# Weight sums of two more pairs kept in DRAM, the leftover GpSimd jobs run under the output projection, and attention's transposes placed inside the next chunk's products

## The chip, the cores and the metric

The kernel runs on one core of a Trainium2 chip. The metric is the device time of one execution, in microseconds (us). The kernel before takes 1067.46 us as the median of 3 runs (1066.02 to 1068.29).

The engines of the core have short names in everything below: PE is TensorE (matrix products and transposes), DVE is VectorE, ACT is ScalarE, POOL is GpSimd, and SP is the engine whose queue issues most of the DMA transfers. Each engine works through its own list of instructions in order, and waits on the others by semaphores. L235 is line 235 of the kernel before, unless a line is said to be of the kernel after.

## What is computed

One encoder layer over 1024 positions of 1024 features, all in fp32:

```python
def reference(x, ...):
    h = rmsnorm(x, norm_mix_pre)
    y = mixer(h, w_in, conv_a, ...)            # 8 groups of short convolution, 4 heads of gated linear attention
    x = x + rmsnorm(y @ w_out, norm_mix_post)  # (w_out is inside mixer)
    h = rmsnorm(x, norm_ffn_pre)
    u = dwconv3(h @ w_up, conv_ffn)            # 1024 -> 2 * 2816, then a convolution of width 3 over positions
    gate, val = split(u)
    y = (silu(gate) * val) @ w_down            # 2816 -> 1024
    return x + rmsnorm(y, norm_ffn_post)
```

Attention works in chunks of 64 positions, forward and backward: a chunk's decayed keys `k_out` times its values give a state update `kv`, the states are scanned along the chunks, and the output is the masked scores times the values plus the queries times the state before.

## The kernel before, in words

Every fp32 operand of a large product is split into a high and a low part (ACT copies the high part, DVE subtracts to get the low part), and a product is three passes on PE: high by high, high by low, low by high. The whole program is bound to PE's list, which runs through these stages:

- **Start, 0 to 111 us.** Norm of x, its transposes (`hT`), the projection to V, and four output gates (`swish_gate`).
- **Attention and short convolution, 111 to 326 us.** `gla_head` (a generator, L474 on) is run for four heads, and its parts are interleaved with `conv_tile`, whose large products (`pgc`, `pgv`, `pgb`) are made by `feature_chunk` (L226 on): eight k-steps of 6 matmuls each, and after every k-step one entry of the list `between` is taken off and called. `gla_head` puts the state products (`states`) and the scores into that list. Two kinds of transposes on PE stand outside it: the decayed keys (`cum`, made by DVE at L514) are transposed into `pko` (L519) and copied to `koT`; the normed head output (`on`, made by DVE at L616) is transposed into `pot` (L622) and multiplied into `yT` by DVE.
- **The border, 326 to 440 us.** `w_out_tile(t)` multiplies one tile of 128 rows by w_out (PE, 8 tiles), then ACT and DVE norm it twice; `h2_transpose(t)` turns the result for the next stage. The weights of the up projection's first pairs are loaded and split here (`begin`, which makes `ug0h` and `ug0l` and so on).
- **Up projection, 440 to 849 us.** 22 pairs of a gate block and a value block, `up(c)`, pair c from 0 to 21. A pair is made by a scheme of seven block products instead of eight, each of 12 matmuls of 128x512, and needs four sums of weight blocks, s1 to s4. ACT, DVE and POOL prepare pair c+1 while PE works on pair c. DVE has besides the splits the additions of products into `cg` and `cv` (L1015, L1029, L1032, L1040, L1043), which read a bank of PE's output and free it for the next product, the convolution (L990, L991), the product of gate and value (L1066), and for odd pairs four sums (L1078 to L1082) of the activations, stored to DRAM.
- **Down projection, 849 to 1059 us**, a scheme of seven products too, over activations and weight sums in DRAM; then the last norm.

Where the weight sums come from: `jobs` is a list of 15 side jobs for POOL. Four of them (`up_begin`, `up_end`) load blocks of w_up, make four sums of 128x512 and store them to DRAM (`wu_d`), for pairs 0 to 3. Eleven (`down_begin`, `down_end`) do the same for w_down. `side()` starts one job and ends the one begun before. It is called during the start and the output gates; at L1160 a `while jobs` loop runs the three that are left, after the first product of the down projection. Pairs 0 to 3 (`N_EARLY = 4`) load their sums in `begin_sums`. For pairs 4 to 21 `make_sums(c)` (L868 on) loads the two full blocks (`ug4r`, `uv4r` for pair 4) and POOL makes the sums `us40r`, `us41r` (L880 to L883) two pairs ahead, in `up(c - 2)`.

A name as `us3al` is read so: weight sums of pair 3, s2 and s3 (`a`; `b` is s1 and s4), low part. `us30r` and `us31r` are the raw fp32 sums.

Of the kernel before, what the change touches and what calls it, by code (L numbers as in the profile page):

```python
# [40 lines left out]
def kernel(  # L41
# [39 lines left out]
    def ps_tile(name):  # L81
        return psp.tile([P, 1024], F32, tag="ps", name=name)
# [21 lines left out]

    def up_end(k, ag, av):
# [25 lines left out]

    def late_tile(name):
        return sp.tile([P, D], F32, tag="r", name=name)

    jobs = [(up_begin, up_end, i) for i in range(4)] + [(down_begin, down_end, q) for q in range(NQ)]

# [142 lines left out]
    with ExitStack() as n1:  # L279
# [133 lines left out]
        nc.tensor.transpose(pp[:, P : P + NPB], stk[0:NPB, 1, :], ident[0:NPB, 0:NPB])  # L413
        nc.vector.tensor_copy(prm, pp[:, 0 : P + NPB])

# [20 lines left out]
    nc.sync.dma_start(out=up_raw[RANK : 2 * RANK, :, DK:P], in_=gate_up_bwd[0].rearrange("r (h d) -> r h d", d=DK))  # L436
    nc.vector.tensor_copy(up96[0:32], up_raw)
    nc.vector.tensor_copy(up96[32:64], up_raw)
    nc.vector.tensor_sub(up96[64:96], up_raw, up96[0:32].bitcast(F32))

# [24 lines left out]
    def unit(tag, name, dt=F32, bufs=1):  # L465
        return mp.tile([P, L], dt, tag=tag, name=name, bufs=bufs)
# [8 lines left out]
    def gla_head(h):  # L475
# [40 lines left out]

        pk = ps_tile(f"pko{h}")
        for t in range(NT):
            nc.tensor.transpose(pk[:, t * P : (t + 1) * P], cum[:, t * P : (t + 1) * P], ident)  # L519
        koT = unit("koT", f"koT{h}")  # L520
        nc.scalar.copy(koT, pk)
# [22 lines left out]
        def states(i):  # L544
# [73 lines left out]

        pt = ps_tile(f"pot{h}")
        ptv = pt.rearrange("p (a b c i) -> p a b c i", b=2, c=2, i=CH)  # L620
        for s in range(NT):
            nc.tensor.transpose(ptv[:, s % 4, :, s // 4, :], on[:, s * P : (s + 1) * P], ident)  # L622
        nc.vector.scalar_tensor_tensor(yT[4 + h], pt, g_head, yT[4 + h], op0=ALU.mult, op1=ALU.mult)

# [370 lines left out]
    def up(c, before=iter(())):  # L995
# [268 lines left out]
```

## Time and profile before

| | |
|---|---|
| median of 3 runs | 1067.46 us (1066.02 to 1068.29) |
| the profiled execution: its own time | 1067.92 us |
| the profiled execution: span of the core | 1065.9 us |
| mean granted PE clock | 0.995 |
| PE busy | 98% of the span |
| DVE busy | 74% |
| ACT busy | 44% |
| POOL busy | 24% |

The profile is of one execution. 2.0 us of its own time lie outside of the span. Views of it that are used below: the waits of PE (each row a pair of the instruction that waited and what it waited for, with the total, the number of waits and the longest), the table by windows (busy time of PE, PE's weight loads, DVE, ACT, POOL in a stretch of time, each with its count of instructions, then the granted clock, the share of the DMA engines and GB/s), and the timelines of one engine: the start, the duration, the engine, the line, the operation, output <- inputs, the shape, a count, and in brackets the idle time before it and what ended it. Durations on PE overlap, since matmuls are pipelined; the difference of two starts is the time that PE gave to one.

### The profile page before, as it was taken

How to read it: one execution, taken by the hardware profiler on the slowest of the kernel's cores; microseconds unless marked ns; L12 is line 12 of the kernel's file. 1: busy time of each engine (PE TensorE's matmuls, PEld its weight loads, DVE VectorE, ACT ScalarE, POOL GpSimd, SP SyncE). 2: the span in 40 equal slices, each digit the busy share in tenths (PEclk: the TensorE clock that was granted, in tenths of full speed). 3: DMA queues.
4: the chain of work that ended last, by engine and by line, in shares of the span. 5: the costliest groups of instructions: out<-in, count | busy, mean ns of one | idle time of the engine just before them, and what ended most of it. 6: DMA issues, size and time to landing. Idle time of an engine off the chain costs nothing.

```text
span 1065.9 us, 14084 instructions
## 1 busy us (share of the span) xinstructions
PE 1048.0 (98%) x5409; PEld 873.1 (82%) x5409; DVE 789.9 (74%) x991; ACT 466.0 (44%) x636; POOL 255.2 (24%) x236
## 2 busy tenths in 40 slices
PE   8999999999999999998999999999999999999997
PEld 7998878778888888887788888888888888888886
DVE  6951479789868457989888987977987885545575
ACT  5431354553435334653444434444344554343442
POOL 2798820000000000014423433242240007200011
PEclk9999999999999999998999999999999999999999
DMA  8788720210156222252333323223332679966555
GB/s 289 274 277 301 237 93 20 60 41 21 40 179 187 80 80 79 89 148 93 104 94 118 117 89 109 99 89 109 120 108 90 205 274 350 334 214 199 171 173 202
DMA packets 124212, 158.70 MB, mean 149 GB/s; under 512 B 15841, under 2 KB 83570, under 8 KB 124146
## 3 DMA queue, kind: packets, MB, share of 16 engines
q1 hardware_dynamic: 113634, 119.80, 35.1%
q0 software_dynamic: 9936, 36.18, 9.3%
q10 hardware_dynamic: 576, 1.84, 0.4%
q8 instruction: 42, 0.69, 0.3%
q14 instruction: 24, 0.20, 0.1%
HBM read 113.49 MB, written 44.30 MB: 148 GB/s over the span
## 4 chain that ended last, share of the span: by engine, by line
PE 85%; DVE 9%; issue 2%; DMA 2%; ACT 1%; POOL 0%; SPq 0%; DVEq 0%; POOLq 0%; ACTq 0%
PE pb L810 14%; PE pdb L1132 10%; PE pc L810 9%; PE pa L810 9%; PE pw L740 8%; PE pgc L235 4%; PE pgo L235 4%; PE pv L346 4%; PE pgv L235 3%; PE pqk L235 3%; PE pdd L1132 3%; PE pdc L1132 3%; PE pda L1132 3%; PE pgb L235 2%; PE pdl L1132 1%
## 5 line engine op out<-in xcount | busy, mean ns | idle before, releaser
L1132 PE MATMUL pdb<-d 128*128 128x512 f32 (+1 forms) x495 | 109.3, 382 | 0.0
L1132 PEld LDWEIGHTS pdb<-d 128*128 128x128 f32 x495 | 90.8, 188 | 18.1
L880 POOL TENSOR_TENSOR us41r<-uv4r 128x512 f32<-128x512 f32 x1 | 2.1, 2113 | 326.1 <-DVE uv L991 326.1
L810 PE MATMUL pb<-t,uv 128*128 128x512 f32 x264 | 63.6, 390 | 1.2 <-DVE cv L1032 1.2
L810 PEld LDWEIGHTS pb<-t,uv 128*128 128x128 f32 x264 | 49.4, 188 | 11.9 <-DVE cv L1032 1.6
L1063 ACT ACTIVATE uu<-uu 128x1024 f32<-128x1024 f32 x22 | 23.4, 1062 | 43.3 <-DVE uu L991 43.3
L1015 DVE TENSOR_TENSOR cg<-cv,pb 128x512 f32<-128x512 f32 x22 | 15.0, 682 | 36.1 <-ACT uu L989 19.0
L990 DVE SCALAR_TENSOR_TENSOR uv<-cv,prm,uv 128x1023 f32<-128x1023 f32 x22 | 32.3, 1470 | 0.0
L1021 ACT COPY cg<-pa 128x512 f32<-128x512 f32 x22 | 12.9, 586 | 43.5 <-PE pa L810 43.5
L990 DVE SCALAR_TENSOR_TENSOR uu<-cg,prm,uu 128x1023 f32<-128x1023 f32 x22 | 31.1, 1415 | 0.0
L571 DVE SCALAR_TENSOR_TENSOR S<-S,dec 64x128 f32<-64x128 f32 x56 | 19.3, 344 | 14.6 <-ACT S L562 12.3
L1132 PE MATMUL pdc<-d 128*128 128x512 f32 x132 | 30.1, 389 | 0.0
L1132 PE MATMUL pdd<-d 128*128 128x512 f32 x132 | 30.1, 389 | 0.0
L991 DVE SCALAR_TENSOR_TENSOR uv<-cv,prm,uv 128x1023 f32<-128x1023 f32 x22 | 29.1, 1321 | 0.0
L1132 PEld LDWEIGHTS pdc<-d 128*128 128x128 f32 x132 | 24.8, 188 | 5.1
L1132 PEld LDWEIGHTS pdd<-d 128*128 128x128 f32 x132 | 24.8, 188 | 5.1
L991 DVE SCALAR_TENSOR_TENSOR uu<-cg,prm,uu 128x1023 f32<-128x1023 f32 x22 | 28.9, 1313 | 0.0
L989 ACT ACTIVATE uu<-cg,prm 128x1024 f32<-128x1024 f32 x22 | 25.2, 1145 | 6.6 <-DVE as L1081 3.6
L1183 POOL DMA_DIRECT2D x2r<-x2d x4 | 2.1, 534 | 106.2 <-DMA d_8r<-actd 96.4
L1066 DVE TENSOR_TENSOR uu<-uu,uv 128x1024 f32<-128x1024 f32 x22 | 27.2, 1236 | 0.0
L989 ACT ACTIVATE uv<-cv,prm 128x1024 f32<-128x1024 f32 x22 | 25.4, 1154 | 2.9 <-DVE as L1081 2.1
L901 ACT COPY cv<-pa 128x512 f32<-128x512 f32 x22 | 12.8, 589 | 29.4 <-PE pa L810 29.4
(1190 smaller groups left out, 3146.3 us busy)
## 6 DMA issues: line engine op xcount, KB each, us to landing
actd<-as SPq DMA_DIRECT2D x20, 512.0 KB, 2.7
x<-in_x_dram SPq DMA_DIRECT2D x16, 512.0 KB, 5.7
actd<-uu SPq DMA_DIRECT2D x10, 512.0 KB, 3.7
x2d<-x SPq DMA_DIRECT2D x8, 512.0 KB, 3.3
actd<-uu SPq DMA_DIRECT2D x10, 256.0 KB, 2.0
out_dram<-o POOLq DMA_DIRECT2D x5, 512.0 KB, 7.0
x2r<-x2d POOLq DMA_DIRECT2D x4, 512.0 KB, 3.9
x2r<-x2d SPq DMA_DIRECT2D x4, 512.0 KB, 4.0
```

The costliest lines, as they stand in the source:

```text
L235: nc.tensor.matmul(o[hf], wt[:, k, :], act[hf][a][:, k, :], start=(k == 0 and wt is wh and a == 0), stop=(k == KT - 1 and wt is wl))
L346: keep(nc.tensor.matmul(ps[:, n * 512 : n * 512 + VH], a[:, k, sl], w[:, k % 2, n * VH : (n + 1) * VH], start=(j == 0), stop=(j == 3 * KT ...
L571: nc.vector.scalar_tensor_tensor(S[0:DK, c + 1, :], S[0:DK, c, :], dec[0:DK, c : c + 1], S[0:DK, c + 1, :], op0=ALU.mult, op1=ALU.add)
L740: ins = nc.tensor.matmul(ps[:, n * HALF : (n + 1) * HALF], a[:, k, sl], w[:, n * HALF : (n + 1) * HALF], start=(i == 0 and q == 0), stop=( ...
L810: nc.tensor.matmul(o, w[:, k, :], m[:, k, :], start=start and k == 0 and q == 0, stop=k == 3 and q == 2, skip_group_check=True)
L989: nc.scalar.activation(u, src, AF.Copy, scale=ffn_tap(1, r))
L990: nc.vector.scalar_tensor_tensor(u[:, 1:L], src[:, 0 : L - 1], ffn_tap(0, r), u[:, 1:L], op0=ALU.mult, op1=ALU.add)
L991: nc.vector.scalar_tensor_tensor(u[:, 0 : L - 1], src[:, 1:L], ffn_tap(2, r), u[:, 0 : L - 1], op0=ALU.mult, op1=ALU.add)
L1015: nc.vector.tensor_add(cg[:, hi], cv[:, lo], pb)
L1063: last_act[0] = nc.scalar.activation(ug, ug, AF.Silu)
L1066: nc.vector.tensor_mul(ug, ug, uv)
L1132: nc.tensor.matmul(o, a[:, 0, sl], b[:, 1, r], start=start and i == 0, stop=stop and i == 2, skip_group_check=True)
```

## The change

1. **The jobs.** After the eighth w_down job two new ones stand in the list, for pairs 4 and 5: `pair_begin` loads the two full blocks of w_up (two transfers each), `pair_end` makes the four sums (the same four operations as `up_end`, now in `block_sums`) and stores them to DRAM, `wu_p`. The five jobs that the start doesn't reach (pairs 4 and 5, then the last three of w_down) run in the border: `side` is called once behind `split_y(1)`, once behind each of `w_out_tile(1)` to `(4)`, and once more. Their tiles come from the pool `wpool`, ahead of its use by the up projection's weights. The loop at L1160 is gone.
2. **The pairs.** Pairs 4 and 5 load their sums from `wu_p` in `begin_sums` (`N_DRAM = 6`); their full gate block, for `split_gate`, is loaded by SP in `up(2)` and `up(3)`. `make_sums` begins with pair 6, called in `up(3)`, a pair earlier in the loop than before; from `up(5)` on it is called for pair c+2 as before.
3. **The transposes.** `decayed` (the `pko` transposes and the copy to `koT`) is put at the head of `between`, and `outputs` (the `pot` transposes and the product into `yT`) of heads 0 to 2 is appended to it, so that they are called behind the first and the second k-step of the next chunk; the states follow behind the third. The last head's `outputs` is called at once, as before.
4. **The order of the first splits.** The splits of `ug0`, `ug1`, `ug2` and of pair 0's sums are put behind the norm of row tiles 3, 4 and 5; three small DVE copies (`up96`) behind the copy of the parameters.

```diff
+    wu_p = {c: dramp.tile([P, 4, 4, P], F32, tag="wup", name=f"wup{c}", bufs=2) for c in (4, 5)}
...
+    def pair_begin(c, tile, after):
+        t = [tile(f"wp{c}{x}") for x in "gv"]
+        for o, w in zip((c, NFC + c), t):
+            if after is not None:
+                nc.gpsimd.tensor_copy(w[:, 0:1], after)
+            v = w.rearrange("p (k n) -> p k n", n=P)
+            for ks in (slice(0, 4), slice(4, KT)):
+                load = nc.gpsimd.dma_start(out=v[:, ks], in_=w_up[:, ks, o * P : (o + 1) * P])
+        loads.append(load)
+        return [w.rearrange("p (a n) -> p a n", a=2) for w in t]
+
+    def pair_end(c, ag, av):
+        block_sums(ag, av)
+        nc.gpsimd.dma_start(out=wu_p[c][:, 1:3].rearrange("p a k n -> p a (k n)"), in_=av)
+        nc.gpsimd.dma_start(out=wu_p[c][:, 0:4:3].rearrange("p a k n -> p a (k n)"), in_=ag)
...
-    jobs = [(up_begin, up_end, i) for i in range(4)] + [(down_begin, down_end, q) for q in range(NQ)]
+    jobs = [(up_begin, up_end, i) for i in range(4)] + [(down_begin, down_end, q) for q in range(8)]
+    jobs += [(pair_begin, pair_end, c) for c in (4, 5)] + [(down_begin, down_end, q) for q in range(8, NQ)]
...
-        between.append(lambda: None)
+        between.insert(0, decayed)
+        if h == 0:
+            between.append(lambda: None)
...
+        if h + 1 < HEADS:
+            between.append(outputs)
+        else:
+            outputs()
...
     split_y(1)
+    side(border_tile, ident[:, 0:1], ahead=1)
     for t in range(1, 5):
         w_out_tile(t)
+        side(border_tile, ident[:, 0:1], ahead=1)
+    side()
...
-        if n < N_EARLY:
+        if n < N_DRAM:
             begin_sums(n, 1)
-        if N_EARLY <= c + 2 < NFC:
-            make_sums(c + 2)
+        if N_EARLY <= c + 2 < N_DRAM:
+            g = (sp, cvp)[c % 2].tile([P, KT, P], F32, tag="r", name=f"ug{c + 2}r")
+            nc.sync.dma_start(out=g, in_=w_up[:, :, (c + 2) * P : (c + 3) * P])
+            pair[c + 2] = {"rg": g}
+        m = c + 3 if c + 3 == N_DRAM else c + 2 if c + 2 > N_DRAM else NFC
+        if m < NFC:
+            make_sums(m)
...
-    while jobs:
-        side(late_tile if len(jobs) % 3 == 0 else spare_tile, y[0][:, 0:1])
```

On PE in attention, second head: before, the transposes `pot` of head 0 and `pko` of head 1 stand between two chunks, `pqk` (the queries and keys of head 2) and `pgc`.

```order
L235 MATMUL pqk_1740<-hTl_106,qk2h 128x512
L235 MATMUL pqk_1740<-hTh_103,qk2l 128x512
L235 MATMUL pqk_1740<-hTh_105,qk2l 128x512
L622 MATMUL pot_1795<-ident,on_1718 128x2x64 x8
L519 MATMUL pko_1805<-ident,cum_1607 128x128 x8
L235 MATMUL pgc_1823<-hTh_103,gc1h 128x512
L235 MATMUL pgc_1823<-hTh_105,gc1h 128x512
```

And now, from the last rows of the first k-step of `pgc` to the states:

```order
L257 MATMUL pgc_1804<-hTh_107,gc1l 128x512
L546 MATMUL pko_1811<-ident,cum_1609 128x128 x8
L257 MATMUL pgc_1804<-hTh_105,gc1h 128x512
L257 MATMUL pgc_1804<-hTh_107,gc1h 128x512
L257 MATMUL pgc_1804<-hTl_106,gc1h 128x512
L257 MATMUL pgc_1804<-hTl_108,gc1h 128x512
L257 MATMUL pgc_1804<-hTh_105,gc1l 128x512
L257 MATMUL pgc_1804<-hTh_107,gc1l 128x512
L651 MATMUL pot_1828<-ident,on_1720 128x2x64 x8
```

The 16 transposes are the same ones; `pko` comes one k-step of 6 matmuls later than before, `pot` two and behind `pko`.

On POOL, behind the job of `wd14r` and `wd15r` (the last that runs in the start), before: the sums of pairs 4 and 5, then of pair 6, in the up projection.

```order
L130 DMA wdd_87<-wd15r 128x1024
L880 TENSOR_TENSOR us41r<-uv4r 128x512
L882 TENSOR_TENSOR us50r<-ug5r,uv5r 128x512
L881 TENSOR_TENSOR us40r<-us41r,ug4r 128x512
L882 TENSOR_TENSOR us40r<-ug4r,uv4r 128x512
L883 TENSOR_TENSOR us41r<-ug4r,us40r 128x512
L880 TENSOR_TENSOR us51r<-uv5r 128x512
L881 TENSOR_TENSOR us50r<-us51r,ug5r 128x512
L883 TENSOR_TENSOR us51r<-ug5r,us50r 128x512
L880 TENSOR_TENSOR us61r<-uv6r 128x512
```

The end of the five border jobs on POOL and what now follows them:

```order
L148 TENSOR_TENSOR wd21r<-wd21r,wd20r 128x512
L151 DMA wdd_92<-wd20r 128x1024
L149 TENSOR_TENSOR wd21r<-wd21r 128x512
L151 DMA wdd_92<-wd21r 128x1024
L925 TENSOR_TENSOR us61r<-uv6r 128x512
L926 TENSOR_TENSOR us60r<-us61r,ug6r 128x512
L927 TENSOR_TENSOR us60r<-ug6r,uv6r 128x512
L928 TENSOR_TENSOR us61r<-ug6r,us60r 128x512
```

The sums of pairs 4 and 5 are gone from POOL's list in the up projection, and pair 6's are the first there.

On SP, behind the load of `uv3r` in the up projection, before:

```order
L828 DMA uv3r<-in_w_up_dram 128x4x128
L876 DMA ug5r<-in_w_up_dram 128x8x128
L876 DMA uv5r<-in_w_up_dram 128x8x128
L1072 DMA actd_3968<-uu_4126 128x512
L876 DMA ug6r<-in_w_up_dram 128x8x128
L1075 DMA actd_3968<-uu_4235 128x1024
L1083 DMA actd_3968<-as_4272 128x1024
L1084 DMA actd_3968<-as_4273 128x1024
L1072 DMA actd_3969<-uu_4348 128x512
L876 DMA uv6r<-in_w_up_dram 128x8x128
```

And after, where `wup` holds the sums of pairs 4 and 5 and `actd` the stored activations:

```order
L873 DMA uv3r<-in_w_up_dram 128x4x128
L1052 DMA ug5r<-in_w_up_dram 128x8x128
L904 DMA us40r<-wup_80 128x512 x2
L904 DMA us41r<-wup_80 128x512 x2
L1126 DMA actd_4034<-uu_4192 128x512
L873 DMA uv4r<-in_w_up_dram 128x4x128
L921 DMA uv6r<-in_w_up_dram 128x8x128
L1129 DMA actd_4034<-uu_4293 128x1024
L904 DMA us50r<-wup_81 128x512 x2
L1137 DMA actd_4034<-as_4330 128x1024
L1138 DMA actd_4034<-as_4331 128x1024
L904 DMA us51r<-wup_81 128x512 x2
```

Eight transfers of sums have joined the queue; `uv4r` and `uv5r` are loaded as halves (128x4x128), and `uv6r` is issued ahead of the second activation store of pairs 0 and 1 (row L1129), where it stood behind the first of pairs 2 and 3.

More of the change, by code (lines that the diff above doesn't have):

```diff
@@ L103, in up_begin, with block_sums @@
         return t
-    def up_end(k, ag, av):
+    def block_sums(ag, av):
         nc.gpsimd.tensor_add(av[:, 1], av[:, 0], av[:, 1])
@@ L413 @@
         nc.tensor.transpose(pp[:, P : P + NPB], stk[0:NPB, 1, :], ident[0:NPB, 0:NPB])
-        nc.vector.tensor_copy(prm, pp[:, 0 : P + NPB])
+        prm_in = nc.vector.tensor_copy(prm, pp[:, 0 : P + NPB])
         pt = ps_tile("plr")
@@ L436 @@
     nc.sync.dma_start(out=up_raw[RANK : 2 * RANK, :, DK:P], in_=gate_up_bwd[0].rearrange("r (h d) -> r h d", d=DK))
-    nc.vector.tensor_copy(up96[0:32], up_raw)
-    nc.vector.tensor_copy(up96[32:64], up_raw)
-    nc.vector.tensor_sub(up96[64:96], up_raw, up96[0:32].bitcast(F32))
+    with tc.issue_after(prm_in.ins):
+        nc.vector.tensor_copy(up96[0:32], up_raw)
+        nc.vector.tensor_copy(up96[32:64], up_raw)
+        nc.vector.tensor_sub(up96[64:96], up_raw, up96[0:32].bitcast(F32))
     mask = gp.tile([P, 2, CH], I32, tag="mask", name="mask")
@@ L515, in gla_head, with decayed @@
         yield
[L517 to L521, printed above, removed]
         A = gp.tile([P, HALF], F32, tag="A", name=f"A{h}")
         tiles = {}
+        def decayed():
+            pk = ps_tile(f"pko{h}")
+            for t in range(NT):
+                nc.tensor.transpose(pk[:, t * P : (t + 1) * P], cum[:, t * P : (t + 1) * P], ident)
+            tiles["koT"] = unit("koT", f"koT{h}")
+            nc.scalar.copy(tiles["koT"], pk)
         def scores(i):
@@ L553, in states @@
                 o0 = par * HALF + (c8 // 2) * DV
-                nc.tensor.matmul(kv[:, o0 : o0 + DV], koT[r, t * P : (t + 1) * P], V[t][r, h * DV : (h + 1) * DV],
+                nc.tensor.matmul(kv[:, o0 : o0 + DV], tiles["koT"][r, t * P : (t + 1) * P], V[t][r, h * DV : (h + 1) * DV],
                                  start=True, stop=True)
@@ L617, in gla_head, with outputs @@
         yield
[L619 to L623, printed above, removed]
+        def outputs():
+            pt = ps_tile(f"pot{h}")
+            ptv = pt.rearrange("p (a b c i) -> p a b c i", b=2, c=2, i=CH)
+            for s in range(NT):
+                nc.tensor.transpose(ptv[:, s % 4, :, s // 4, :], on[:, s * P : (s + 1) * P], ident)
+            nc.vector.scalar_tensor_tensor(yT[4 + h], pt, g_head, yT[4 + h], op0=ALU.mult, op1=ALU.mult)
+        if h + 1 < HEADS:
+            between.append(outputs)
+        else:
+            outputs()
     def conv_tile(j, last):
@@ L728, with behind @@
     hn = [None] * NT
+    normed = [None] * NT
+    def behind(t):
+        stack = ExitStack()
+        for ins in normed[t]:
+            stack.enter_context(tc.issue_after(ins.ins))
+        return stack
     def w_out_tile(t):
@@ L752, in w_out_tile @@
         ss = small.tile([P, 1], F32, tag="ss", name=f"ssx{t}")
-        nc.scalar.activation(tmp, x2, AF.Square, accum_out=ss)
+        normed_a = nc.scalar.activation(tmp, x2, AF.Square, accum_out=ss)
         rs = rstd_of(ss, D)
-        nc.vector.scalar_tensor_tensor(tmp, x2, rs[:, 0:1], g2, op0=ALU.mult, op1=ALU.mult)
+        normed[t] = normed_a, nc.vector.scalar_tensor_tensor(tmp, x2, rs[:, 0:1], g2, op0=ALU.mult, op1=ALU.mult)
     b1 = []
@@ L788 @@
     split_y(1)
+    side(border_tile, ident[:, 0:1], ahead=1)
     for t in range(1, 5):
         w_out_tile(t)
+        side(border_tile, ident[:, 0:1], ahead=1)
+    side()
+    assert not jobs and not begun
     h2_transpose(0)
@@ L849 @@
     pair = {}
-    N_EARLY = 4
+    N_EARLY, N_DRAM = 4, 6
     def begin_sums(c, ring=2):
         t = pair.setdefault(c, {})
-        g = wu_d[:, :, :, c * P : (c + 1) * P]
+        g = wu_d[:, :, :, c * P : (c + 1) * P] if c < N_EARLY else wu_p[c]
         t["r23"], t["r14"] = (raw_tile([P, 2, 4, P], f"us{c}{i}r", ring) for i in range(2))
@@ L883, in make_sums, with begin @@
         nc.gpsimd.tensor_sub(s4, t["rg"][:, 4:8], s2)
-    def begin(c):
+    def begin(c, t=None):
         pair[c] = {}
-        pair[c]["a11"], pair[c]["a12"] = split_gate(c, load_gate(c, 0))
+        raw = load_gate(c, 0)
+        with ExitStack() if t is None else behind(t):
+            pair[c]["a11"], pair[c]["a12"] = split_gate(c, raw)
     def bank(name):
@@ L908, in early_cv @@
         return cvp.tile([P, D], F32, tag="r", name=f"cv{c}")
-    begin(0)
-    begin(1)
+    begin(0, 3)
+    begin(1, 4)
     w_out_tile(6)
     h2_transpose(4)
-    begin(2)
+    begin(2, 5)
     begin_sums(0, 0)
-    pair[0]["s2"], pair[0]["s3"] = split_sums(0, pair[0]["r23"], "a")
-    pair[0]["s1"], pair[0]["s4"] = split_sums(0, pair[0]["r14"], "b")
+    with behind(5):
+        pair[0]["s2"], pair[0]["s3"] = split_sums(0, pair[0]["r23"], "a")
+        pair[0]["s1"], pair[0]["s4"] = split_sums(0, pair[0]["r14"], "b")
     w_out_tile(7)
```

6 lines of the change are left out of this document (4 added, 2 removed).

## The prediction, as put on record before the kernel ran

> **What bounds the kernel now.** The page first: how much of the span belongs to PE.
>
> ```profile
> span 1065.9 us, 14084 instructions
> PE 1048.0 (98%) x5409; PEld 873.1 (82%) x5409; DVE 789.9 (74%) x991; ACT 466.0 (44%) x636; POOL 255.2 (24%) x236
> ```
>
> The change takes no matmul away, so it can only give back PE's idle time and PE's slow time. The waits of PE say what there is, with the reader's line, what it waited for, the total, the number and the longest:
>
> ```profile
> PE pb L810 <- DVE cg L1015: 3.3, 1, 3.3
> ...
> PE pot L622 <- DVE on L616: 1.5, 1, 1.5
> PE pb L810 <- DVE cv L1032: 1.2, 1, 1.2
> ...
> PE pot L622 <- ACT gv2h L193: 0.7, 1, 0.7
> PE pko L519 <- PE pqk L235: 0.5, 1, 0.5
> ```
>
> The table by windows says where (after the window's length: busy PE, PE's weight loads, DVE, ACT, POOL, then the granted clock):
>
> ```profile
> 140.00:190.00 50.00, 48.03 (x353) 38.92 (x352) 43.21 (x63) 26.53 (x34) 0.00 (x0) 1.00 0.20 54
> ...
> 326.00:406.00 80.00, 80.00 (x371) 66.66 (x371) 47.29 (x85) 29.75 (x64) 0.00 (x0) 1.00 0.34 116
> ...
> 489.00:535.00 46.00, 41.43 (x168) 32.80 (x167) 41.13 (x38) 17.28 (x19) 16.18 (x10) 0.93 0.34 119
> 535.00:849.00 314.00, 314.00 (x1387) 259.84 (x1386) 267.05 (x268) 134.71 (x150) 90.41 (x56) 1.00 0.33 110
> ```
>
> From 535 on PE has no gap, and none in the border (326 to 406). What is to be had lies in two places: attention, and 489 to 535, where PE is idle for 4.6 us and the clock is 0.93. There PE's timeline reads so:
>
> ```profile
> 481.72 2.88 PE L810 MATMUL pb<-t,uv 128*128 128x512 f32 x12
> 484.44 0.39 PE L810 MATMUL pb<-t,us3ah 128*128 128x512 f32 x1
> ...
> 489.43 0.39 PE L810 MATMUL pc<-t,us3bl 128*128 128x512 f32 x1
> 493.15 1.22 PE L810 MATMUL pb<-t,us3ah 128*128 128x512 f32 x2 [3.34 <-DVE cg L1015]
> ...
> 498.44 0.60 PE L810 MATMUL pa<-b1h,ug4h 128*128 128x512 f32 x1
> ```
>
> Twelve matmuls undisturbed take 2.72 us from start to start (481.72 to 484.44), 0.227 each. The twelve from 493.15 to 498.44 take 5.29. So one wait of 3.34 cost 498.44 - 489.43 = 9.01 us where 0.23 + 2.72 = 2.95 were due: **6.1 us**, of which about 2.5 are the slow clock behind the wait.
>
> Why was the cg addition late? DVE's timeline:
>
> ```profile
> 472.22 1.21 DVE L1066 TENSOR_TENSOR uu<-uu,uv 128x1024 f32<-128x1024 f32 x1
> ...
> 476.94 1.27 DVE L991 SCALAR_TENSOR_TENSOR uv<-cv,prm,uv 128x1023 f32<-128x1023 f32 x1
> ...
> 478.74 1.71 DVE L991 SCALAR_TENSOR_TENSOR uu<-cg,prm,uu 128x1023 f32<-128x1023 f32 x1
> ...
> 480.96 1.72 DVE L694 TENSOR_TENSOR ug4l<-ug4r,ug4h 128x1024 fp32r<-128x1024 f32 x1
> ...
> 483.21 1.71 DVE L1066 TENSOR_TENSOR uu<-uu,uv 128x1024 f32<-128x1024 f32 x1
> 484.96 2.19 DVE L694 TENSOR_TENSOR us4al<-us40r,us4ah 128x1024 fp32r<-128x1024 f32 x1
> ...
> 487.67 1.48 DVE L1078 TENSOR_TENSOR as<-uu,uu 128x512 f32<-128x512 f32 x1
> 489.07 1.76 DVE L1079 TENSOR_TENSOR as<-uu 128x512 f32<-128x512 f32 x1
> 490.76 1.74 DVE L1081 TENSOR_TENSOR as<-as,uu 128x512 f32<-128x512 f32 x1
> 492.42 0.67 DVE L1015 TENSOR_TENSOR cg<-cv,pb 128x512 f32<-128x512 f32 x1
> 493.02 0.68 DVE L1082 TENSOR_TENSOR as<-uu,as 128x512 f32<-128x512 f32 x1
> ```
>
> Each kind has a fast row (1.21 for a 128x1024 operation, 1.27 for the convolution's, 0.68 for 128x512) and a slow one. The slow ones lose 0.44 + 0.51 + 0.50 + 0.98 + 0.80 + 1.08 + 1.06 = 5.4 us, all of them between 478.7 and 492.5, while POOL makes the eight sums of pairs 4 and 5. One of these, and the first and last of pair 6's four:
>
> ```profile
> 479.32 2.28 POOL L881 TENSOR_TENSOR us40r<-us41r,ug4r 128x512 f32<-128x512 f32 x1
> ...
> 509.19 1.29 POOL L880 TENSOR_TENSOR us61r<-uv6r 128x512 f32<-128x512 f32 x1 [17.24 <-DMA uv6r<-in_w_up_dram]
> ...
> 514.06 2.15 POOL L883 TENSOR_TENSOR us61r<-ug6r,us60r 128x512 f32<-128x512 f32 x1
> ```
>
> That POOL's sums slow DVE is my reading of rows that coincide; the second wait has the same shape. POOL's four sums of pair 6 run from 509.19 to 516.2, and the three convolution rows of DVE in that time, here the first and the last, take 2.3 to 2.4 where 1.27 is fast; they lose 1.1 each or less, 3.2 in all:
>
> ```profile
> 510.44 2.37 DVE L990 SCALAR_TENSOR_TENSOR uv<-cv,prm,uv 128x1023 f32<-128x1023 f32 x1
> ...
> 514.98 2.31 DVE L991 SCALAR_TENSOR_TENSOR uv<-cv,prm,uv 128x1023 f32<-128x1023 f32 x1
> ```
>
> Then cv (L1032) is 1.2 late.
>
> **Part 1, transposes.** Removed: the waits 1.5, 0.7 and 0.5 of pot and pko, 2.7 us, with what it takes PE to start again. The one of 1.5:
>
> ```profile
> 185.19 0.62 PE L235 MATMUL pqk<-hTl,qk2h 128*128 128x512 f32 x2
> 185.65 0.61 PE L235 MATMUL pqk<-hTh,qk2l 128*128 128x512 f32 x2
> 187.73 1.06 PE L622 MATMUL pot<-ident,on 128*128 128x128 f32 x8 [1.47 <-DVE on L616]
> 188.63 1.04 PE L519 MATMUL pko<-ident,cum 128*128 128x128 f32 x8
> 189.42 0.70 PE L235 MATMUL pgc<-hTh,gc1h 128*128 128x512 f32 x2
> 189.97 0.63 PE L235 MATMUL pgc<-hTl,gc1h 128*128 128x512 f32 x2
> ```
>
> Two matmuls take 0.46 (185.19 to 185.65), so pot was due at 186.11 and came 1.62 later, 0.15 over its wait. With 0.15 for each of the three, 3.1 us go. The cover: a k-step of 6 matmuls is 3 x 0.46 = 1.4 us, so pko is due 1.4 later, over its wait of 0.5; pot is due behind two k-steps and the 0.8 of pko, 3.6 later, over 1.5. What they feed is not due earlier: the states stand a k-step behind. Added: the break in a chunk. After transposes two matmuls take 0.55 (189.42 to 189.97) against 0.46, and I take as much for the way in: 0.2 for a break. Before there was one break for pot and pko together, now there are two, for three heads (the first has no pot ahead of it, the last head's pot stays): 3 x 0.2 = 0.6. Bounds: 0 (the weights load under the matmuls) and 1.2 (twice my price). Sum: **-2.5**.
>
> **Part 2, the sums of pairs 4 and 5 leave the up projection.** The eight POOL sums go from that stretch. DVE's 5.4 us go with them: the cg addition would start at 492.42 - 5.4 = 487.0, and PE wants its result at 489.43 + 0.23 = 489.66. With its 0.6 it is 2.0 early, so the wait goes, and with it the slow clock: -6.1. The wait of 1.2 at L1032, from pair 6's sums at that place, goes too as they move: -1.2, with restart **-7.4** for both.
>
> [...]
>
> What is late next: pair 6's four sums. They are POOL's first in the stage, and uv6r is loaded earlier. They write into the buffers that cv of pairs 1 and 2 leave, so the first starts when the convolution of pair 2 has read its cv. Counted with fast rows from 487.0, DVE does L1015 and L1082 (0.6 each) and three rows of the convolution (1.2 each), so that is at 491.8; then L1029 of pair 3 is through at 492.4, and behind another 1.2 L1032 at 494.2. PE without its stall reads the first at 489.66 + 2.72 + 2 x 0.227 = 492.8 (a product, and two matmuls of pa as at 498.44) and the second a product later, at 495.5: a slack of 0.4 and 1.3. The slow-down by pair 6's sums is known only between 0 (they start behind L1032) and 3.2 (all of it falls ahead of L1032, as it did before), so the new wait is between 0 and 3.2 - 0.4 = 2.8. I take **+1.0**, nearer to nothing, since the buffers hold the sums back.
>
> **Part 3, the jobs in the border.** 20 sums at 1.29 (the row of 509.19) to 2.28 are 26 to 46 us of POOL, and some 24 issues at 0.57 are 14 more:
>
> ```profile
> 138.98 0.57 POOL L130 DMA_DIRECT2D wdd<-wd15r  x1 [0.41 <-POOL wd15r L128]
> ```
>
> POOL has 80 idle us in 326 to 406 and no other work. What it hits there is DVE, busy for 47.3 of 80: 32.7 us free. At 0.8 lost for each sum (3.2 for four) DVE loses 16, at 1.1 22; both fit, and PE reads nothing there that DVE made less than a row tile (10 us) ago. Who waits: the weights of pair 0 (ug0) take the buffers of the jobs' tiles and wait for their stores; by 13 sums (17 to 30 us) and 17 issues (10) these are out 27 to 40 us after 326, by 366, and PE wants ug0 only behind the eight row tiles, past 406. I cost it at nothing; without that cover of 40 us each us later would be a us of PE. [...]
>
> The loop of three jobs in the down projection goes; no wait of PE is there in the waits, so that gives 0. The two sums' loads on SP for pairs 4 and 5 are new, in front of activation stores; a load of the kind lands in 4.0 us:
>
> ```profile
> us31r<-wud SPq DMA_DIRECT2D x2, 256.0 KB, 4.0
> ```
>
> For pair 4 they stand ahead of the store of the product L1066 of 472.22, so they land by about 476 if their buffers are free, and are split (us4al) at 484.96: 8 us to spare, which a buffer that comes free late may eat. The reordered splits of ug0 to ug2 are three rows of 1.2 on DVE put into those 32.7 us: 0.
>
> **The sum.** -2.5 - 7.4 + 1.0 = -8.9 us. The profiled execution took 1067.92, 0.46 over the median, so 1059.0 against itself and **1058.6** against the median of 1067.46.
>
> **The rivals.** (a) *The transposes gain nothing*: the waits move to what follows them (ACT's koT copy ahead of the states, DVE's work for the next head), as these lie in the same chunk. For it: ACT and DVE are busy for 27 and 43 of the 50 us from 140 to 190. Against it: pko gets a whole k-step of slack. 1058.6 + 2.5 = 1061.1. (b) *The stall comes back in part*: the sums of pair 6 push L1029 or L1032 beyond the wait from which the clock falls, one such stall for 6.1 instead of my 1.0: 1058.6 + 5.1 = 1063.7. For it: DVE is busy for 41 of the 46 us in that window, and the sums now meet its densest part. Against it: the bound of 2.8 is under 3.3. (c) *Slower*: pair 6's sums, made earlier, meet DVE with a backlog and stall PE at both L1029 and L1032 of pair 3 for over 3.3 us each, each with its slow clock: 2 x 6.1 - 1.0 = 11.2, 1069.8. It decides from a wait of 3.3 at both; eight slow rows at 1.1 would be needed ahead of L1032 where three have been seen.
>
> **How the numbers follow.** A measurement of this kernel can tell about 0.2%, 2.1 us, from no change: faster means below 1065.3, slower above 1069.6. Forecast 0.63, (a) 0.15, (b) 0.16, (c) 0.05, and 0.01 for what else lies within 0.2%. Faster: 0.63 + 0.15 + 0.10 of (b) = 0.88; same: 0.06 of (b) and 0.01, 0.07; slower 0.05. The low end: no break and no new wait, 1067.46 - 3.1 - 7.4, less 0.5 for small gaps, 1056.5. The high end takes in (a), the new wait's 2.8 and most of (b): 1064.0; it leaves out (c) and the rest of (b), 0.12.
>
> **What would show it.** Right: no wait of pot or pko in PE's waits; the stretch from 478 to 492 without POOL sums and with DVE rows at 1.2; no wait at L1015 of pair 3, a granted clock of 1.00 there; a PE wait at L1029 or L1032 of at most 3 us; border windows with PE full. Wrong: a wait of 3.3 us or more with a clock below 1.00 in the up projection (b, c); a wait at koT or kv in attention (a); PE waiting for ug0 behind the row tiles; DVE rows as slow as before without POOL sums beside them, by which my cause would fall.

## The result and the profile after

The changed kernel takes 1056.79 us (median of 4 runs, 1056.44 to 1057.15) where the kernel before took 1066.96 beside it (4 runs, 1066.02 to 1068.29): the ratio is 0.9904, with a 95% interval of 0.9887 to 0.9921. That is 10.2 us, and 11.4 us between the two profiled executions (spans 1065.9 and 1054.5; the own time of the second is 1056.59). The forecast was 1058.6 in a range of 1056.5 to 1064.0: the time lies 0.3 us above the low end.

The page of the changed kernel, its span and PE's row:

```profile
span 1054.5 us, 14136 instructions
...
PE 1043.2 (99%) x5409; PEld 871.2 (83%) x5409; DVE 799.3 (76%) x991; ACT 465.7 (44%) x636; POOL 258.4 (24%) x252
```

PE is busy for 4.8 us less than before with as many matmuls, 2.6 of it the slow clock of pair 3 that has gone. The waits of PE behind the start are now these two, where there were 3.3, 1.5, 1.2, 0.7 and 0.5:

```profile
PE pb L855 <- DVE t L728: 0.4, 1, 0.4
PE pc L855 <- DVE cv L1083: 0.2, 1, 0.2
```

The first stands at 437, between the border and the up projection; the second is new and stands in pair 3. A second profiled execution of the same kernel (e12 below) lacks the first and has more of the second:

```profile
PE pc L855 <- DVE cv L1083: 0.8, 1, 0.8
```

The table by windows, for the stretches shown of before:

```profile
140.00:190.00 50.00, 50.00 (x362) 40.84 (x361) 43.81 (x63) 26.54 (x33) 0.57 (x1) 1.00 0.20 55
...
326.00:406.00 80.00, 80.00 (x375) 66.79 (x374) 60.89 (x82) 28.93 (x64) 39.00 (x44) 1.00 0.61 217
...
489.00:535.00 46.00, 45.76 (x203) 37.53 (x202) 41.00 (x42) 19.70 (x22) 13.05 (x8) 1.00 0.33 109
```

PE is full from 140 to 190, full in the border beside 39 us of POOL, and short of full by 0.24 where it was by 4.57. The border row shows 13.6 us more of DVE, but the stage begins 3.25 us earlier now (322.80 for 326.05), so the two rows don't hold the same work. Over the whole stage, from the first pw to the first pb, DVE has 138 instructions in both kernels and is busy for 92.8 us where it was for 76.4: 16.4 more. Taken by the first matmuls of the stages, the 11.4 us come from two places alone:

| from, to (first matmul) | before | after | difference |
|---|---|---|---|
| start, pqk | 111.06 | 110.89 | -0.17 |
| pqk, pw (attention) | 214.99 | 211.91 | -3.08 |
| pw, pb (border) | 113.70 | 113.68 | -0.02 |
| pb, pda (up projection) | 409.24 | 401.10 | -8.14 |
| pda, last matmul (down projection) | 209.75 | 209.75 | 0.00 |

PE's timeline in the second head, where the wait of 1.47 was:

```profile
186.63 1.03 PE L546 MATMUL pko<-ident,cum 128*128 128x128 f32 x8
187.42 0.71 PE L257 MATMUL pgc<-hTh,gc1h 128*128 128x512 f32 x2
187.97 0.62 PE L257 MATMUL pgc<-hTl,gc1h 128*128 128x512 f32 x2
188.43 0.63 PE L257 MATMUL pgc<-hTh,gc1l 128*128 128x512 f32 x2
188.90 1.03 PE L651 MATMUL pot<-ident,on 128*128 128x128 f32 x8
189.69 0.70 PE L257 MATMUL pgc<-hTh,gc1h 128*128 128x512 f32 x2
```

Neither group waits. Two groups take 0.79 each and the pair of matmuls behind each 0.55 (187.42 to 187.97); before, pot took 0.90, pko 0.79 and one pair 0.55. With a pair at 0.45 for the second break that is 2.69 then and 2.68 now: with the wait gone, the second break adds nothing to the sum.

DVE's timeline in the stretch that was slow (L1120 is the L1066 of before, L1069 the cg addition L1015, L1083 and L1086 the cv additions L1029 and L1032, L1039 the convolution):

```profile
479.01 1.22 DVE L1120 TENSOR_TENSOR uu<-uu,uv 128x1024 f32<-128x1024 f32 x1
480.15 1.22 DVE L728 TENSOR_TENSOR us4al<-us40r,us4ah 128x1024 fp32r<-128x1024 f32 x1
...
483.09 0.68 DVE L1135 TENSOR_TENSOR as<-as,uu 128x512 f32<-128x512 f32 x1
483.69 0.68 DVE L1069 TENSOR_TENSOR cg<-cv,pb 128x512 f32<-128x512 f32 x1
484.29 1.19 DVE L1136 TENSOR_TENSOR as<-uu,as 128x512 f32<-128x512 f32 x1
...
488.98 0.68 DVE L1083 TENSOR_TENSOR cv<-cv,pc 128x512 f32<-128x512 f32 x1
489.58 2.10 DVE L1039 SCALAR_TENSOR_TENSOR uu<-cg,prm,uu 128x1023 f32<-128x1023 f32 x1
491.61 0.67 DVE L1086 TENSOR_TENSOR cv<-cv,pb 128x512 f32<-128x512 f32 x1
492.21 1.72 DVE L728 TENSOR_TENSOR us4bl<-us41r,us4bh 128x1024 fp32r<-128x1024 f32 x1
```

And POOL's and PE's beside it, POOL with the last issue of the border and the first, second and last of pair 6's sums:

```profile
376.91 0.57 POOL L151 DMA_DIRECT2D wdd<-wd21r  x1 [0.42 <-POOL wd21r L149]
483.11 1.82 POOL L925 TENSOR_TENSOR us61r<-uv6r 128x512 f32<-128x512 f32 x1 [105.64 <-DMA uv6r<-in_w_up_dram]
489.32 1.28 POOL L926 TENSOR_TENSOR us60r<-us61r,ug6r 128x512 f32<-128x512 f32 x1 [4.39 <-DVE uv L1039]
...
492.81 2.28 POOL L928 TENSOR_TENSOR us61r<-ug6r,us60r 128x512 f32<-128x512 f32 x1
```

```profile
489.09 0.39 PE L855 MATMUL pa<-b1l,ug4h 128*128 128x512 f32 x1
489.71 0.73 PE L855 MATMUL pc<-t,us3bh 128*128 128x512 f32 x2 [0.24 <-DVE cv L1083]
```

The rows that lost 5.4 us before are back at 1.22 and 0.68. Pair 6's first sum slows one row (L1136, 1.19 for 0.68), and this half microsecond, less the slack that was there, is the wait of 0.24 at L1083. In e12 the same first sum starts at 482.55 and meets the row before the cg addition, which loses 1.1 us instead of 0.5:

```profile
482.74 1.78 DVE L1135 TENSOR_TENSOR as<-as,uu 128x512 f32<-128x512 f32 x1
```

The wait at L1083 is 0.83 there, and the cg addition is through 0.7 us ahead of PE's read. So the size of the new wait changes from execution to execution. The other three sums, held back until DVE has read cv of pair 2, slow L1039 to 2.10 and us4bl to 1.72, behind L1083, and PE waits for neither.

### The profile page after: what moved, and what is told of

It reads as the page before. It is cut to its first block, busy times and chain, and to the rows that moved or that the text cites. A ratio compares the mean times of both kernels' runs of the same rounds, so it can differ in the third digit from the quotient of the medians.

```text
span 1054.5 us, 14136 instructions
## 1 busy us (share of the span) xinstructions
PE 1043.2 (99%) x5409; PEld 871.2 (83%) x5409; DVE 799.3 (76%) x991; ACT 465.7 (44%) x636; POOL 258.4 (24%) x252
## 4 chain that ended last, share of the span: by engine, by line
PE 94%; DVE 4%; DMA 1%; issue 0%; ACT 0%; SPq 0%; DVEq 0%; ACTq 0%
PE pb L855 16%; PE pc L855 11%; PE pdb L1186 10%; PE pa L855 10%; PE pw L781 8%; PE pgv L257 4%; PE pgc L257 4%; PE pqk L257 4%; PE pgo L257 4%; PE pv L368 4%; PE pgb L257 3%; PE pdd L1186 3%; PE pdc L1186 3%; PE pda L1186 3%; PE pdl L1186 1%; PE kv L579 1%
## 5 line engine op out<-in xcount | busy, mean ns | idle before, releaser
L1069 DVE TENSOR_TENSOR cg<-cv,pb 128x512 f32<-128x512 f32 x22 | 15.0, 683 | 35.2 <-PE pb L855 17.4
L794 ACT ACTIVATE tmp<-x 128x1024 f32<-128x1024 f32 x8 | 8.5, 1062 | 47.9 <-DVE x L791 47.9
L1039 DVE SCALAR_TENSOR_TENSOR uu<-cg,prm,uu 128x1023 f32<-128x1023 f32 x22 | 28.9, 1312 | 0.0
L1039 DVE SCALAR_TENSOR_TENSOR uv<-cv,prm,uv 128x1023 f32<-128x1023 f32 x22 | 28.1, 1275 | 0.0
L1038 DVE SCALAR_TENSOR_TENSOR uu<-cg,prm,uu 128x1023 f32<-128x1023 f32 x22 | 28.0, 1275 | 0.0
L1120 DVE TENSOR_TENSOR uu<-uu,uv 128x1024 f32<-128x1024 f32 x22 | 27.2, 1238 | 0.1
```

What stands on the lines that cost most here:

```text
L1038: nc.vector.scalar_tensor_tensor(u[:, 1:L], src[:, 0 : L - 1], ffn_tap(0, r), u[:, 1:L], op0=ALU.mult, op1=ALU.add)
L1039: nc.vector.scalar_tensor_tensor(u[:, 0 : L - 1], src[:, 1:L], ffn_tap(2, r), u[:, 0 : L - 1], op0=ALU.mult, op1=ALU.add)
L1069: nc.vector.tensor_add(cg[:, hi], cv[:, lo], pb)
L1120: nc.vector.tensor_mul(ug, ug, uv)
```

## The experiments

Twelve kernels were run; e3, e4, e7, e8 and e9 have one run each. Where an expectation speaks of the changed kernel's time, its 1056.59 to 1056.79 is meant. My theory is that POOL's sums slowed DVE and so stalled PE, and that the transposes' gain stands apart from that. The rivals: the stall came of the order of work or of the loads; the parts help or hinder each other.

**Each part alone.** e1 is the kernel before with this edit alone, e2 the changed kernel with it undone:

```diff
-        pk = ps_tile(f"pko{h}")
...
+        def decayed():
...
+        between.insert(0, decayed)
...
+            between.append(outputs)
```

> The kernel before with the third part of the change alone: pko and pot called behind the first and second k-step of the next chunk; the sums, jobs and splits as before. If the two parts add up and a break in a chunk costs nothing, 3.1 us go, and PE's stage from the first pqk to the first pw takes 211.9 us instead of 215.0; the wait of 3.3 at L1015 of pair 3 and the slow clock behind it stay. By my price of 0.6 for the breaks, 2.5. By the rival (the waits move to koT or to DVE), under 1, and new waits of PE stand in attention.

> The changed kernel with the transposes back between the chunks. If the parts add up, 8.2 us less than the kernel before, all of it between the first pb and the first pda (409.2 us before, 401.1 in the changed kernel), and the waits of pot and pko (1.5, 0.7, 0.5) are back. If the stall of pair 3 hung on attention's timing in any way, the stage would be longer than 401.5 again.

e1: 1063.66 us (6 runs, 1062.99 to 1065.65) against 1067.05, ratio 0.9966 (0.9952 to 0.9980), 3.4 us. Attention takes 211.89 us, and the wait in pair 3 stays:

```profile
PE pb L821 <- DVE cg L1026: 3.3, 1, 3.3
```

e2: 1060.58 us (4 runs, 1060.27 to 1061.14), ratio 0.9941 (0.9924 to 0.9957), 6.5 us where 8.2 was expected. The up projection takes 400.79 us, 8.45 less than before, but attention 215.79, 0.80 more: the wait of pko in the first head is 1.3 where it was 0.5. The view names no engine for it; cum, which pko reads, is DVE's and ends 0.2 us before pko starts (145.43 and 145.64). DVE has a slow row ahead of cum, beside the end of POOL's jobs of the start, which took 1.23 before:

```profile
138.23 2.66 DVE L535 TENSOR_TENSOR qd<-qd,m 128x1024 f32<-128x1024 f32 x1
```

The changed kernel has this row too (2.65, at 138.12), and its pko, a k-step of 1.36 later, does not wait. So the parts nearly add up, 3.4 and 6.5 to the 10.2 of both, and they aren't quite apart: the transposes' new place also hides 0.8 that e2 shows.

**POOL's operations by themselves.** e3, e4 and e8 are the changed kernel with operations of POOL that nobody needs, started by the landing of us41r:

```diff
+        if n == 4:
+            z = t["r14"].rearrange("p a k n -> p (a k n)")
+            for i in range(10):
+                nc.gpsimd.tensor_add(scr, z[:, 0:384], z[:, 512:896])    # e3
+                nc.gpsimd.tensor_copy(scr, z[:, 0:384])                  # e8
+            for i in range(24):
+                nc.gpsimd.memset(scr, 0.0)                               # e4, behind one addition
```

> The changed kernel and, when pair 4's loaded sums us41r have landed (about 472), ten additions of 128x384 on POOL that read us41r and write a scratch tile nobody reads; nothing else is moved or loaded. Theory: POOL's operations as such slow DVE's. They run for some 12 to 17 us, DVE's rows with two operands in SBUF lose 0.4 to 1.1 us each beside them, 4 to 6 us in all, against a slack of 2.0 at the cg addition of pair 3 (L1069): PE waits 2 to 4 us there or at L1083 behind it, the clock falls behind a wait of 3.3, and the time grows by 2 to 7 us. Rival: the stall of the kernel before came of the order of the work or of the loads, not of POOL; then DVE's rows stay at 1.2 and 0.68 and the time within 1 us of the changed kernel's.

> As the run with ten additions, but one addition and then 24 memsets of the same scratch tile on POOL, which read nothing. If it is POOL's reading of SBUF that stands against DVE's second operand, DVE's rows beside the memsets keep their fast times and the time is the changed kernel's within 1 us. If any work of POOL in SBUF slows DVE, the rows lose as much as with the additions, for as long as the memsets run.

> As the run with ten additions, but ten copies of 128x384 on POOL, which read one operand and write the scratch tile. Additions of two operands cost 6.3 us, memsets of none 0.9. If any read of POOL stands against DVE's second operand, DVE's rows beside the copies lose as much as they did beside the additions (0.2 to 0.8 each), for as long as the copies run. If it takes POOL's second operand, they keep 1.2 and 0.68 and the time is within 1 us of the changed kernel's.

e3 took 1063.08 us, 6.3 more. POOL, DVE and PE of that run:

```profile
472.61 16.84 POOL L1054 TENSOR_TENSOR scr<-us41r 128x384 f32<-128x384 f32 x10 [97.49 <-DMA us41r<-wup]
```

```profile
480.87 2.03 DVE L728 TENSOR_TENSOR us4al<-us40r,us4ah 128x1024 fp32r<-128x1024 f32 x1
482.82 0.67 DVE L1102 TENSOR_TENSOR cv<-cv,pb 128x512 f32<-128x512 f32 x1
...
485.67 1.50 DVE L1140 TENSOR_TENSOR as<-as,uu 128x512 f32<-128x512 f32 x1
...
488.51 2.03 DVE L1039 SCALAR_TENSOR_TENSOR uv<-cv,prm,uv 128x1023 f32<-128x1023 f32 x1
490.46 2.30 DVE L1039 SCALAR_TENSOR_TENSOR uu<-cg,prm,uu 128x1023 f32<-128x1023 f32 x1
```

```profile
487.83 0.73 PE L855 MATMUL pb<-t,us3ah 128*128 128x512 f32 x2 [1.12 <-DVE cg L1074]
...
494.61 0.89 PE L855 MATMUL pc<-t,us3bh 128*128 128x512 f32 x2 [3.31 <-DVE cv L1088]
495.29 0.63 PE L855 MATMUL pc<-t,us3bl 128*128 128x512 f32 x1
495.72 1.06 PE L855 MATMUL pc<-t,us3bh 128*128 128x512 f32 x2
```

The stall is back, with its slow clock, and POOL's additions are all that was added. The wait of 1.12 at the cg addition is theirs alone. The one of 3.31 at L1088 (the L1029 of before) is theirs and pair 6's: its first sum stood behind them in POOL's list, ran at 489.42 instead of 483.11, and slowed the row of 2.30. Of DVE's rows beside them, those with two operands in SBUF are slow (us4al 2.03 for 1.22), and those that read one from PE's output (cv, from pb) keep 0.67. In e4 (1057.53, inside the changed kernel's own runs of 1056.37 to 1057.57) DVE's rows beside the memsets are as fast as without them:

```profile
474.02 11.38 POOL L1056 MEMSET scr<- 128x384 f32 x24
```

```profile
480.53 1.22 DVE L728 TENSOR_TENSOR us4al<-us40r,us4ah 128x1024 fp32r<-128x1024 f32 x1
```

What is slow in e4 stands beside additions: its one addition and pair 6's first sum, which starts at 485.36, slow a convolution row each (2.04 and 2.31 for 1.28), and PE's waits at L1090 (the L1083 of the changed kernel) are 1.1 in all. Copies, e8 (1058.31), slow DVE's rows too:

```profile
480.97 1.52 DVE L728 TENSOR_TENSOR us4al<-us40r,us4ah 128x1024 fp32r<-128x1024 f32 x1
```

So in these runs DVE's rows with two operands in SBUF lost time beside operations of POOL that read SBUF (us4al, 1.22 in the changed kernel, took 2.03 beside the additions and 1.52 beside the copies), and not beside memsets, which only write it (1.22). Over the same five rows, from L1040 (uv) to us4al, 2.2 us are lost beside the additions and 1.3 beside the copies; three of the five lose a little more beside the copies, so it is not shown that the number of operands read is what matters. The times of e4 and e8 alone would prove little, being within 1.6 us of the changed kernel's; the rows do.

**The border's cover.** e7 does the sums of the five border jobs twice or three times over, in effect as shown here (the sums then hold other values, and so does the output); e6 puts pairs 6 and 7 through DRAM too, seven jobs in the border:

```diff
-        block_sums(ag, av)                # e7: n = 2, 3, and so for the w_down jobs 8 to 10
+        for _ in range(n): block_sums(ag, av)
...
-    N_EARLY, N_DRAM = 4, 6                # e6
+    N_EARLY, N_DRAM = 4, 8
```

> The changed kernel with the sums of pairs 6 and 7 through DRAM as well: seven jobs in the border instead of five, POOL's first sums in the up projection are pair 8's. If pair 6's sums are what is left of the stall, the waits of 0.24 at L1083 of pair 3 and the break behind it go, 0.4 us, and the cover of the border (POOL ends at 377 now, 17 us later with two jobs more, ug0 wanted at 415) holds: 0.0 to 0.5 us less than the changed kernel, about 10.5 less than the kernel before. By the rival the border's cover is used up: PE waits for ug0 to ug2 between 415 and 421, and the time grows by 1 to 8 us against the changed kernel.

> The changed kernel with the four sums of each of the five border jobs done twice over, so that the values are not the weights' sums and the output is another. POOL has 20 sums more, 26 us; it ends near 403 instead of 377. DVE, 60.9 busy of 80 us from 326 to 406, loses another 13 or so, and still fits. By the cover as I counted it PE waits for nothing new: within 1 us of the changed kernel. By the rival, DVE's delay reaches PE through the row tiles' norms, and PE waits at the h2 transposes.

> The same with the sums done three times over: 52 us more of POOL than in the changed kernel, end near 429. The buffers of ug0 are free after the third job, some 31 us later than now (near 395), those of ug1 and ug2 after the fourth and fifth, near 420 and 429, but PE wants ug1 at 418 and ug2 behind it: PE waits 5 to 15 us there, and the time grows by as much. If the cover were larger than I counted, or the buffers went to other weights, no change. DVE would need 27 us more than now where 19 are free, so it would be late too.

In all three the border's cover was used up, in e6 and in the tripled e7 by more than the expectations gave (8 and 15 us at most), and PE's waits are not for ug0 to ug2 themselves. e6: 1081.44 us (4 runs), ratio 1.0124 (1.0107 to 1.0141), 14 us slower than the kernel before. e7: 1071.49 and 1089.78, 15 and 33 us over the changed kernel. In e6 the place is ACT's list, and PE's wait follows:

```profile
395.69 1.04 ACT L727 CAST ug0h<-ug0r 128x1024 fp32r<-128x1024 f32 x1 [23.04 <-POOL wd20r L146]
```

```profile
PE tx L809 <- DVE b1l L728: 15.1, 1, 15.1
```

ug0h was next on ACT at 372.6 and its buffer was still a job's: ACT stood for 23 us, with the norms of the row tiles behind it in its list. PE wants the weights only at 415 in the changed kernel, but ACT wanted the buffer at 372. The row names POOL's sum of wd20r, which ended at about the same time. The six buffers are taken in turn, by which ug0h takes that of wd16r; its store was issued at 391.89 and landed in 3.6 us, just ahead of 395.69. In e7 with doubled sums it is DVE that starves. Its addition of x, 1.23 when left alone, with POOL adding almost without a pause:

```profile
394.28 5.83 DVE L792 TENSOR_TENSOR x<-tmp,x 128x1024 f32<-128x1024 f32 x1
```

PE then waits seven times between 390 and 435, 0.2 to 3.8 us each. With tripled sums the longest of its waits is 10.1.

**The order of the first splits.** e9 takes away the fourth part of the change for ug0 to ug2, as shown here, and for pair 0's sums; the three small copies stay:

```diff
-        with ExitStack() if t is None else behind(t):
-            pair[c]["a11"], pair[c]["a12"] = split_gate(c, raw)
+        pair[c]["a11"], pair[c]["a12"] = split_gate(c, raw)
```

> The changed kernel without the fourth part for ug0 to ug2 and pair 0's sums: their splits are no longer put behind the norms of row tiles 3 to 5, and ACT has ug0h between the two squares of row tile 0, ug1h and ug2h in row tile 1. They write into buffers of the border jobs, which are stored to DRAM from about 358 to 380 in the changed kernel. If ACT's place in its own list decides, ACT stands at ug0h from about 335 to 367 and holds up the norms of the row tiles behind it; four banks pairs of PE's output are full after four row tiles (366), so that PE waits 5 to 25 us in the border and the time grows by as much or more, with slow clock behind the waits. By the prediction's count, in which the order of these splits was worth 0 and ug0 had a cover of 40 us, the time stays within 1 us of the changed kernel's.

1072.43 us, 15.6 more. ACT, and the waits of PE:

```profile
357.35 1.05 ACT L727 CAST ug0h<-ug0r 128x1024 fp32r<-128x1024 f32 x1 [21.79 <-POOL wd20r L146]
...
370.90 1.05 ACT L727 CAST ug1h<-ug1r 128x1024 fp32r<-128x1024 f32 x1 [10.89 <-DMA wdd<-wd18r]
```

```profile
PE tx L809 <- DVE tmp L790: 6.0, 1, 6.0
PE pw L781 <- DVE tmp L790: 5.2, 1, 5.2
```

The second row names what ACT waits for by name: the store of a job's tile, wd18r, whose buffer ug1h takes. In the changed kernel ug0h comes at 378.68, behind the second norm of row tile 3, and waits for nothing. The few lines that only put splits later are what makes room for the jobs.

**The leftover jobs, and a version with four pairs.** e10 leaves the three jobs of w_down in their old loop; e11 does that and puts pairs 4 to 7 through DRAM; e12 is the changed kernel beside e11.

```diff
-    for t in range(1, 5):
-        w_out_tile(t)
-        side(border_tile, ident[:, 0:1], ahead=1)
-    side()
+    w_out_tile(1)                         # e11: tiles 1 to 3, N_DRAM = 8
+    side(border_tile, ident[:, 0:1], ahead=1)
+    end, i, st = begun.pop(0)
+    end(i, *st)
+    for t in range(2, 5):
+        w_out_tile(t)
...
+    while jobs:
+        side(late_tile if len(jobs) % 3 == 0 else spare_tile, y[0][:, 0:1])
```

> The changed kernel with only the sums of pairs 4 and 5 in the border, and the three jobs of w_down that are left over back in the loop behind the first product of the down projection, as in the kernel before. If the leftover jobs cost nothing where they were, the time is the changed kernel's within 0.5 us, 10 us under the kernel before, and DVE in the border is less busy (326 to 406: 60.9 us in the changed kernel, 47.3 before) by about the share of 12 of its 20 sums, to about 53. If their place mattered, 1 us or more comes back in the down projection (209.75 us from pda to the last product in both kernels).

> The sums of pairs 4 to 7 through DRAM, their four jobs in the border, and the three leftover jobs of w_down late, as in the kernel before: seven jobs in the border lost 15 us at ug0h's place in ACT's list, and the late place of the leftover jobs cost nothing, so four pairs alone may fit. In ACT's list ug0h stands behind the norm of row tile 3, about 378; by the job of pair 5, whose tiles it takes, its buffer is free near 370, ug1h's (pair 6) near 380 against 389, ug2h's (pair 7) near 391 against 400. If that holds, PE is full in the border, the wait at L1083 of pair 3 goes, and the time is 0 to 0.8 us under the changed kernel's, which is in this call too; what pair 8's sums cost in pair 5 (1.4 and 0.2 us of waits in the run with seven jobs) may take all of it back. By the rival POOL is late, ACT stands at ug0h or ug1h, and the time grows by 5 us or more.

> The changed kernel itself, unaltered, beside the run with four pairs through DRAM: 0.990 of the kernel before.

e10: 1057.19 us (4 runs, 1057.04 to 1057.32), ratio 0.9909 (0.9893 to 0.9926): the changed kernel's time with 12 of its 20 border sums gone (DVE 51.3 us busy from 326 to 406). Moving the leftover jobs into the border gained nothing that these runs can tell. e11: 1058.97 (5 runs, 1058.25 to 1059.83), ratio 0.9926 (0.9913 to 0.9940), against 1057.23 (4 runs, 1056.37 to 1057.57) of e12, ratio 0.9909 (0.9896 to 0.9923): 1.7 slower. The border held (PE's last pw stands at 414.1 in both), but waits came back:

```profile
PE pb L860 <- DVE cv L1091: 1.2, 1, 1.2
PE pa L860 <- ACT cv L953: 0.9, 1, 0.9
```

The first is at pair 5, beside the sums that POOL now makes first, pair 8's, with one of 0.34 behind it; the wait at pair 3 (0.24 and, in e12, 0.83) went and these came two pairs on. The second is between the border and the up projection. No kernel was faster than the changed one.

## Why the prediction was right, and where not

**The transposes.** Forecast -3.1 for the waits and +0.6 for the breaks; measured -3.08 in the stage, and 3.4 us (2.1 to 5.1 by the interval) in e1 by itself. The waits went as worked out. The price of the breaks, 0.2 for each of three, was 0 in sum: the 0.09 behind a group of transposes is real, but pot, no longer behind a wait, took as much less itself. The cover of pko, a k-step against a wait of 0.5, was thinner than it looked, since the same wait can be 1.3 (e2).

**The stall.** Forecast -7.4 for both waits and the slow clock; the stage gave 8.14 with a new wait in it. The cause was argued from rows that coincided (of the eight sums, seven ran beside the slow rows; the first, at 465.64, ran ahead of them), and e3 and e4 show it: additions on POOL bring the stall back (a wait of 3.31 in e3), memsets don't (PE's waits of 1.1 in e4 stand behind additions). The cg addition is through 1.8 us before PE reads it (484.37 against 486.14), forecast 2.0; in e12 it is 0.7.

**The new wait.** Forecast +1.0 out of 0 to 2.8; it is 0.24 and 0.16 of restart in one execution, and 0.83 and 0.16, as much as forecast, in e12. The place was right (L1083, the L1029 of before), and so was the slack of 0.4, in fact 0.27. The way to it was not: only the buffer of cv of pair 2 held sums back, the first sum ran ahead at 483.11, where I had all four from 491.8, and it alone makes the wait, while the three others came behind L1083. That the size came near is in part luck: it hangs on which row of DVE that sum meets.

**The sum.** Between the two profiled executions the gain is 11.4, and 8.9 was forecast. Of the 2.5 between them, 0.6 are the breaks, 0.6 the new wait, and 0.5 small gaps that I counted only at the low end (0.3 at 478.35, 0.2 at 532.79). The second stall is another 0.4: from 517.52 to 524.86 PE took 7.34 us for 25 matmuls that take 5.67 undisturbed, so 1.67 went where 1.3 was counted. The start gave 0.2 that was not forecast.

**The border.** That it costs nothing was right: 113.70 and 113.68. The reason given was wrong. "PE wants ug0 only behind the eight row tiles, past 406 ... that cover of 40 us" took PE's need for the deadline. The deadline is ug0h's turn on ACT, 378.68, against the buffer of a job (wd16r) whose store was issued at 357.68 and landed in 5.7 us: a cover of 15 us. 15.6 us were lost where the turn came earlier (e9), 25 where the jobs took longer (e6). "The reordered splits of ug0 to ug2 ... 0" was the wrong step of the sum: with the jobs in the border that order is worth 15.6 us. The forecast came out because both were in the change. DVE's loss over the stage, 16.4 us, was at the low end of the 16 to 22 that I gave, but "both fit" compared totals; doubled sums (e7) would by totals have fitted too, 92.8 and another 16.4 in the 113.7 of the stage, and cost 15 us by holding up single rows of the norms.

**The clock.** I had the slow clock set in from a wait of 3.3, as it did behind the one of 3.34 in the kernel before and not behind those of 1.47 and 1.17; that it takes so long a wait was my estimate. In e6 it set in after 2.06:

```profile
444.15 0.50 PE L857 MATMUL pa<-b1h,ug0h 128*128 128x512 f32 x1 [2.06 <-ACT cv L950]
...
445.30 0.63 PE L857 MATMUL pa<-b1h,ug0h 128*128 128x512 f32 x1
445.72 0.63 PE L857 MATMUL pa<-b1l,ug0h 128*128 128x512 f32 x1
```

Eight transposes and a single matmul stand just ahead of this wait. In e7 with doubled sums the granted clock was 0.96 from 360 to 406, and 0.52 from 394 to 397, behind waits of only 0.80 and 1.55, with eight transposes between them. So the bound of 2.8 for the new wait was no safeguard against rival (b), as I had used it; what kept it away was that three of the four sums came late. Rivals (a) and (c) did not come about. e3 shows something near (c): POOL's additions ahead of two reads of pair 3, with a wait at both, but at the cg addition and L1029 and not at L1029 and L1032.

## What to carry to other kernels

Work put on an idle engine can be paid by another that runs beside it, as DVE paid here for POOL's sums (5.4 us in the up projection before, 16.4 us in the border now): look for rows of one kind that are slow only in some stretch, and at what ran beside them. A buffer lent to a side job has its deadline where the next writer stands in its engine's list, not where its data is wanted; everything behind the writer waits too (in e6 ACT stood for 23.04 us at ug0h, and PE's wait behind it was 15.1). When one such collision is taken away the next sums of the same kind are the first to look at, since they may only move it (in e11 the wait at pair 3 went, and one of 1.2 at pair 5 came).

## What the runs showed of the hardware

- DVE's rows with two operands in SBUF were slowed by POOL's operations that read SBUF: a 128x1024 row of 1.22 us took 1.48 to 1.52 beside copies (e8) and 1.44 to 2.03 beside additions (e3), and one of 1.23 took 5.83 beside additions almost without pause (e7). DVE's 128x512 rows with one operand in PE's output (0.67 to 0.68 beside the additions of e3) and DVE beside memsets (1.21 to 1.22 for 128x1024, e4) lost nothing.
- The slow clock behind a wait cost differently from run to run: in the kernel before twelve matmuls took 5.29 us after 3.34 of idling, 0.427 each from the third on (granted clock 0.51 from 493 to 499); seven took 0.427 each after 3.33 in e1, seven after 3.31 in e3, and seven after 2.06 in e6. Waits of 1.47 and 1.17 in the kernel before were followed by none (1.00 from 184 to 192 and from 516 to 526), and in e7 two waits of 0.80 and 1.55 close together were (0.52 from 394 to 397). What decides between them is not shown.
